# Dense products of a hybrid attention block: high and low parts in half precision with scaled weights, in place of a rounded 32-bit type

## The chip, the cores and the metric

The kernel runs on one core of a Trainium2 chip. The metric is the time of one execution on the device, in microseconds. Three runs of the kernel before took 1757.48, 1761.77 and 1765.3 us; the median, 1761.77, is the time before. A trace of one execution is read beside it.

A core has five engines that work at the same time, each through its own list of instructions in order: TensorE (matmul, PE in the profile, with its weight loads as PEld), VectorE (DVE), ScalarE (ACT), GpSimd (POOL) and SyncE (SP), which here issues the DMAs. They wait for each other through semaphores. SBUF holds the operands, and matmuls write to PSUM, which has eight banks of 512 columns in 32-bit.

## The reference

One layer of a block with two branches over 1024 tokens of width 1024, in 32-bit arithmetic. Cut to what matters here:

```
h = rms_norm(x, norm_mix)
u = h @ w_in                                  # 1024 x 5144 columns
q, kc, vc, ks, vs, kw, vw, gl, rw, merge = split(u)
o_nsa  = nsa(q, kc, vc, ks, vs, kw, vw, gl)   # attention: compressed, selected, window
o_rwkv = rwkv7(rw)                            # token shift, then a scan over the tokens
g = sigmoid(merge)
y = g[0] * (o_nsa @ proj_nsa) + g[1] * (o_rwkv @ proj_rwkv)
x = x + y @ w_out
n = rms_norm(x, norm_ffn)
a, b = split(causal_conv3(n @ ffn_up))        # 5632 columns, depthwise, three taps
x = x + (silu(a) * b) @ ffn_down              # 2816 rows
```

The dense products are `@ w_in`, the two projections, `@ w_out`, `@ ffn_up` and `@ ffn_down`.

## The kernel before, in words

**How a dense product is made.** Activations lie transposed, 128 channels on the partitions and 512 tokens (one half of the sequence) along the columns. Both operands of a product are split: `hi` is the value rounded to FR, a rounded 32-bit type that TensorE takes in a single pass, and `lo` is what is left over, again in FR. A product is then three passes, hi x hi, hi x lo and lo x hi, added up in one PSUM bank (`mm3`, line 263; `mm3s`, line 272, does two outputs at once). For 1024 input channels that is 3 x 8 = 24 matmuls of 128 x 128 weights by 512 columns per output group of 128 and half.

**Splitting.** ACT copies the 32-bit tile to `hi`; VectorE or POOL subtracts `hi` from the tile to make `lo`. `wload` (line 249) does this for weights: it loads a raw tile of 128 x 1024, ACT makes whi (line 256), and line 258 makes wlo, on VectorE, because the counter `wk` never leaves the range `WK = (0, 200)`. In the FFN, `wraw` (line 1561) loads a raw tile into one of four buffers in turn and `split8` (line 1567) and `cut` (line 1721) split it, mostly on POOL (lines 1572 and 1723).

**The stages, in order of time.**
- To about 60 us: x is loaded, normed (`normed`, line 238) and split into hhi and hlo for both halves; the first two column groups of w_in are loaded.
- To about 690 us: attention (`attention`, line 542). Keys are made and compressed (`kphase`), the values in natural order by `vnat` (line 497, matmuls at line 512 of 280 columns), then for every head the scores (lines 580, 641, 643), the exponentials (lines 650 and 651) and the product with the values (lines 655 to 660). The attention's own operands are half precision already. Between its steps the fillers are put: `zproj` and `mproj`, the other column groups of w_in (line 268), and `prelude`, which prepares the scan.
- To about 1000 us: the scan of the second branch, in eight units of 128 tokens (`front` and `back`), in 32-bit. Its steps wait for each other, and a list of dense work is put between them: the rest of `mproj`, `nproj` and `rproj` (the projections), `wout0` (w_out for the first half), `norm0`, and `ffn0` (the first FFN columns for the first half).
- To about 1215 us: the same for the second half, `gated` at line 1446, w_out at line 1473, and six FFN column pairs (i below NE = 6) with `mm3`.
- To about 1524 us: the other 16 column pairs. Here a 2 x 2 scheme with seven products instead of eight is used for the two halves and the two halves of the channels (`prod`, line 1633: twelve matmuls at line 1636 per product, 84 per pair). `prep_up` (line 1587) makes sums of raw weights on VectorE (lines 1592 to 1598) and splits them. Results are combined by VectorE (lines 1665 to 1682), convolved (`taps`, line 1500: an ACT eviction at line 1502, then VectorE at line 1505) and gated (`silu`, lines 1513 to 1515).
- To the end: the down projection, in five `plain` steps of two row groups (line 1746) and three `combined` steps of four (seven products again, line 1817). Each result is added from PSUM to a running sum by VectorE (`tick`, lines 1748 and 1826).

**What sets the order.** The program is written against a tile framework, which lays down the instructions of each engine in one list by simulated time and by priorities. `tc.cur_priority` gives the attention or the scan the first claim and the fillers the later ones; `tc.issue_after` forces single instructions behind others. `ps` (line 211) hands out PSUM banks by tag: P, M, A and B have two each. A tile with a tag and `bufs=n` waits for the last reader of the tile that had its place n tiles ago.

Of the kernel before, what the change touches and what calls it, by code (L numbers as in the profile page):

```python
# [54 lines left out]
NPOOL = ()  # L55
# [26 lines left out]
      "hlo_5", "hlo_6", "hlo_7")  # L82
CW = -0.5 * float(np.exp(-0.5))
# [83 lines left out]
def build(tc, D, dbg=None, upto=99):  # L167
# [7 lines left out]
    with ExitStack() as ctx:  # L175
# [14 lines left out]
        load(par, D["par"])  # L190

# [24 lines left out]
        def ktiles(p, name):  # L216
            return [p.tile([128, 512], FR, name=f"{name}_{k}", tag=f"{name}_{k}") for k in range(8)]
# [20 lines left out]
        def normed(h, xs, gname, rstd, hi, lo, tmp):  # L238
            for k in range(8):
# [3 lines left out]
                (G if k in NPOOL else V).tensor_sub(ks_(lo[h], k), hf, ks_(hi[h], k).bitcast(F32))  # L243
# [86 lines left out]
        V.tensor_scalar(pd[:, 26:30], par[:, o:o + 4], -0.5, 1.0, op0=ALU.mult, op1=ALU.add)  # L330
        ast = ExitStack()
# [74 lines left out]
        def kphase():  # L406
# [24 lines left out]
            for kv in range(2):  # L431
# [4 lines left out]
                def ev(h, pj):  # L436
                    for g in range(2):
                        for r in range(2):
                            dst = zp[g][64 * r:64 * r + 64, :, 1 + 32 * h:33 + 32 * h]
                            src = pj[64 * g:64 * g + 64].rearrange("p (n l r) -> p l n r", l=8, r=2)[:, :, :, r]  # L440
                            if r == g:
                                A.activation(dst, src, AF.Copy)
                            else:
                                V.tensor_copy(dst, src)
# [52 lines left out]
        def vnat():  # L497
# [3 lines left out]
            wnh = tmp.tile([128, 8, 280], FR, name="wnh", tag="wnh")  # L501
            wnl = tmp.tile([128, 8, 280], FR, name="wnl", tag="wnl")
            A.activation(wnh, wn, AF.Copy)
            G.tensor_sub(wnl, wn, wnh.bitcast(F32))
            for t in range(8):
# [8 lines left out]
                for j, vt in ((0, Vs), (1, Vw)):  # L514
                    src = pn[:, 128 * j:128 * j + 128].rearrange("p (g d) -> p g d", g=2)
                    A.activation(vt[:, t, :, 0:64], src, AF.Copy)
                    V.tensor_sub(vt[:, t, :, 65:129], src, vt[:, t, :, 0:64])
                A.activation(gat[:, t], pn[:, 256:280], AF.Exp, scale=-1.0)
# [167 lines left out]
        def zproj(gi):  # L686
            last = FP["f"].tile([128, 1], F32, name="zlast", bufs=2)

            def ev(h, pj):
                z = FP["f"].tile([128, 512], F32, name="zs", bufs=NZS)  # L690
                A.activation(z, pj, AF.Copy, scale=pd[:, gi:gi + 1])
                V.scalar_tensor_tensor(z[:, 1:512], pj[:, 0:511], P("mu", gi), z[:, 1:512],  # L692
# [3 lines left out]
                else:  # L696
                    V.scalar_tensor_tensor(z[:, 0:1], last, P("mu", gi), z[:, 0:1], op0=ALU.mult, op1=ALU.add)
# [20 lines left out]
        def reload(src):  # L718
            hi, lo = ktiles(FP["h"], "hhi"), ktiles(FP["h"], "hlo")
            for k in range(8):  # L720
# [3 lines left out]
                V.tensor_sub(lo[k], t, hi[k].bitcast(F32))  # L724
# [27 lines left out]
        def oprep():  # L752
            ob["hi"] = [FP["h"].tile([128, 512], FR, name=f"ohi{k}", tag=f"hhi_{k}") for k in range(4)]
            ob["lo"] = [FP["h"].tile([128, 512], FR, name=f"olo{k}", tag=f"hlo_{k}") for k in range(4)]
# [4 lines left out]
            for k in range(4):  # L759
# [3 lines left out]
                V.tensor_sub(ob["lo"][k], t, ob["hi"][k].bitcast(F32))  # L763
# [23 lines left out]
        def ysplit(m):  # L787
            def half(tag, name):
                p, n = (FP["f"], {"fu": 3}.get(tag, 1)) if tag in ("fu", "yx") else (FP["h"], 1)
                return p.tile([128, 512], FR, name=f"{name}{m}", tag=tag, bufs=n)  # L790
# [19 lines left out]
        def wout0(m):  # L810
# [5 lines left out]
            V.scalar_tensor_tensor(xr, pj, 0.5, xr, op0=ALU.mult, op1=ALU.add)  # L816
# [12 lines left out]
        def norm0():  # L829
# [10 lines left out]
            for n, k in enumerate(NK):  # L840
                hi[k], lo[k] = (FP["h"].tile([128, 512], FR, name=f"h2{c}0_{k}", tag=HT[2 * n + x]) for x, c in enumerate("hl"))
# [9 lines left out]
                los.append(V.tensor_sub(lo[k], t, hi[k].bitcast(F32)).ins)  # L851
# [576 lines left out]
        yhi = yp.tile([128, 8, 512], FR, name="yhi")  # L1428
# [504 lines left out]
```

## Time and profile before

| | |
|---|---|
| runs, us | 1757.48, 1761.77, 1765.3 (median 1761.77) |
| profiled execution | span 1754.8 us from the first to the last instruction; the page gives no further time of its own for it |
| instructions | 30772 |
| TensorE clock granted, mean | 0.996 |
| DMA | 224.65 MB, mean 128 GB/s |
| HBM | 153.86 MB read, 63.96 MB written |

How to read it. Times are microseconds unless marked ns. In a row of a group stand the line of the code, the engine, the operation, the tile written and the tiles read, the shapes, the count; then the busy time in all and the mean ns of one; then the idle time of the engine just before those instructions and what ended it. In the chain of waits, each row is a start, a length and a group that followed without a gap; the chain is followed back from the last instruction. In the table by stretches each row gives the busy time of each engine between two moments, with the number of instructions in brackets, then the granted clock, the share of the DMA engines and GB/s. Matmuls are pipelined and their ends are modelled: a matmul's own length is longer than the step from its start to the next start, so a pace is read from starts. The type FR is shown as f32 where a matmul reads it and as fp32r where an engine writes it; F16 is f16.

### The profile page before, as it was taken

The page shows a single profiled execution, that of the slowest core. Times are in us where ns is not written, and L with a number is a line of the kernel's source. Part 1 is how long each engine was busy: PE and PEld are TensorE (multiplying, and loading weights), DVE is VectorE, ACT ScalarE, POOL GpSimd, SP SyncE. Part 2 cuts the span into 40 slices and gives each one's busy share as a digit, 9 for nine tenths or more (in the row PEclk, how much of TensorE's full clock was granted, in tenths as well). Part 3 has the DMA queues.
Part 4 walks back from the last instruction along what each step waited for, and adds up shares of the span by engine and source line. Part 5 has one row for each costly group of instructions (what it writes and reads, how often), then busy time and mean ns, then how long its engine had stood idle before and what let it go on. Part 6 is the DMA issues. An engine that isn't in the chain of part 4 may idle for free.

```text
span 1754.8 us, 30772 instructions
## 1 busy us (share of the span) xinstructions
PE 1719.2 (98%) x11856; PEld 1344.9 (77%) x11856; DVE 1249.7 (71%) x2197; ACT 892.5 (51%) x1605; POOL 482.6 (28%) x349
## 2 busy tenths in 40 slices
PE   8999999999999999999999999999999999999998
PEld 5777667766777778887877878787888888888886
DVE  6445677778766648764547585499988888875798
ACT  6574675657557654446545563454344344534430
POOL 1101121120211220010003200113444444757857
PEclk9999999999999999999999999999999999999999
DMA  6242243331343455445445753443222222723402
GB/s 209 91 131 99 76 153 115 103 103 56 117 155 124 133 171 177 140 126 163 149 154 183 257 203 126 132 157 131 90 73 85 94 74 84 243 71 119 132 13 108
DMA packets 124690, 224.65 MB, mean 128 GB/s; under 512 B 16384, under 2 KB 45440, under 8 KB 124416
## 3 DMA queue, kind: packets, MB, share of 16 engines
q1 hardware_dynamic: 124544, 222.69, 39.1%
q8 instruction: 93, 1.52, 0.4%
q14 instruction: 53, 0.43, 0.1%
HBM read 153.86 MB, written 63.96 MB: 124 GB/s over the span
## 4 chain that ended last, share of the span: by engine, by line
PE 81%; DVE 9%; ACT 4%; DMA 4%; issue 2%; SPq 0%; DVEq 0%; ACTq 0%
PE psP L268 25%; PE psM L1636 7%; PE psA L1636 5%; PE psP L1636 5%; PE psA L268 4%; PE psB L268 2%; PE psP L288 2%; PE psM L268 2%; PE psA L641 2%; PE psM L1746 2%; PE psP L1746 2%; PE psA L1746 2%; PE psB L1746 2%; PE psA L643 2%; PE psM L580 1%
## 5 line engine op out<-in xcount | busy, mean ns | idle before, releaser
L268 PE MATMUL psP<-hhi,whi 128*128 128x512 f32 x560 | 227.7, 407 | 0.9 <-DVE zs L692 0.6
L268 PE MATMUL psP<-hlo,whi 128*128 128x512 f32 x560 | 225.4, 403 | 1.7 <-DVE hlo L243 1.7
L258 DVE TENSOR_TENSOR wlo<-wraw,whi 128x1024 fp32r<-128x1024 f32 (+1 forms) x98 | 113.7, 1161 | 73.1 <-ACT whi L256 39.6
L652 DVE TENSOR_TENSOR pl<-pf,ph 128x512 f16<-128x512 f32 (+3 forms) x208 | 118.7, 579 | 60.1 <-ACT pf L651 58.7
L268 PE MATMUL psP<-hhi,wlo 128*128 128x512 f32 x560 | 154.4, 404 | 0.0
L256 ACT ACTIVATE whi<-wraw 128x1024 fp32r<-128x1024 f32 (+1 forms) x98 | 93.0, 953 | 92.1 <-PE psP L268 43.3
L650 ACT ACTIVATE ph<-psA 128x512 f16<-128x512 f32 (+3 forms) x208 | 99.4, 478 | 73.1 <-PE psA L645 43.6
L268 PEld LDWEIGHTS psP<-hhi,whi 128*128 128x128 f32 x560 | 105.4, 188 | 25.1 <-DVE zs L692 1.4
L268 PEld LDWEIGHTS psP<-hlo,whi 128*128 128x128 f32 x560 | 105.5, 188 | 24.8 <-DVE hlo L243 2.7
L587 DVE TENSOR_REDUCE mp<-psM 128x1 f32<-128x512 f32 (+2 forms) x192 | 96.1, 516 | 33.2 <-PE psM L585 25.9
L268 PEld LDWEIGHTS psP<-hhi,wlo 128*128 128x128 f32 x560 | 102.4, 188 | 21.3 <-issue 0.5
L1572 POOL TENSOR_TENSOR wlo<-wraw,whi 128x1024 fp32r<-128x1024 f32 (+1 forms) x33 | 68.1, 2064 | 142.9 <-PE psA L268 46.3
L651 ACT ACTIVATE pf<-psA 128x512 f32<-128x512 f32 (+3 forms) x208 | 99.9, 480 | 0.0
L655 PEld LDWEIGHTS <-ph 128*128 128x128 f16 x592 | 55.8, 96 | 19.6 <-issue 9.3
L660 PEld LDWEIGHTS <-pl 128*128 128x128 f16 x592 | 54.9, 98 | 18.2 <-issue 6.2
L1372 POOL TENSOR_TENSOR b<-b,bonus 128x512 f32<-128x512 f32 x8 | 10.4, 1299 | 203.0 <-ACT b L1370 199.6
L1572 POOL TENSOR_TENSOR s34l<-s,s34h 128x1024 fp32r<-128x1024 f32 x16 | 38.6, 2413 | 93.4 <-ACT s34h L1571 89.9
L674 POOL TENSOR_TENSOR onat<-onat,ot 128x256 f32<-128x256 f32 x32 | 28.1, 885 | 122.6 <-DVE ot L673 85.8
L1515 DVE SCALAR_TENSOR_TENSOR th<-th,u 128x512 f32<-128x512 f32 x38 | 59.5, 1566 | 0.1
L658 PEld LDWEIGHTS <-ph 128*128 128x128 f16 x592 | 56.1, 97 | 2.4 <-issue 1.7
L1571 ACT ACTIVATE whi<-wraw 128x1024 fp32r<-128x1024 f32 (+1 forms) x38 | 33.5, 880 | 42.3 <-PE psP L1636 28.6
L1636 PE MATMUL psP<-h2h,whi 128*128 128x512 f32 x128 | 50.1, 391 | 1.2 <-ACT p L1662 1.2
(819 smaller groups left out, 5124.6 us busy)
## 6 DMA issues: line engine op xcount, KB each, us to landing
wraw<-f_up SPq DMA_DIRECT2D x56, 512.0 KB, 3.5
wraw<-w_t SPq DMA_DIRECT2D x46, 512.0 KB, 3.9
wraw<-f_dn SPq DMA_DIRECT2D x22, 512.0 KB, 4.0
th_d<-th SPq DMA_DIRECT2D x38, 256.0 KB, 2.2
sg_d<-zs SPq DMA_DIRECT2D x32, 256.0 KB, 2.3
wraw<-w_out SPq DMA_DIRECT2D x16, 512.0 KB, 3.4
z_d<-zs SPq DMA_DIRECT2D x28, 256.0 KB, 3.7
x<-xT SPq DMA_DIRECT2D x24, 256.0 KB, 5.9
```

The costliest lines, as they stand in the source:

```text
L256: A.activation(hi[:, :nk], raw, AF.Copy)
L258: (V if WK[0] <= wk[0] < WK[1] else G).tensor_sub(lo[:, :nk], raw, hi[:, :nk].bitcast(F32))
L268: lastm[0] = T.matmul(ps, a[:, k], ks_(b, k), start=(n == 0), stop=(n == 3 * nk - 1)).ins
L587: V.reduce_max(mp[:, x, br, t:t + 1], pm[:, 0:(b1 - b0) * 128], axis=AX.X)
L650: A.activation(ph[0:nkey, rg], pa[0:nkey, rg], AF.Exp, scale=0.125)
L651: A.activation(pf[0:nkey, rg], pa[0:nkey, rg], AF.Exp, scale=0.125)
L652: V.tensor_sub(pl[0:nkey, rg], pf[0:nkey, rg], ph[0:nkey, rg])
L658: T.matmul(pov[:, t, 0:64], ph[0:nkey, tk], vt[0:nkey, kb, g, 65:129], start=False, stop=False, skip_group_check=True)
L1515: V.scalar_tensor_tensor(th, th, 0.5, ub, op0=ALU.mult, op1=ALU.mult)
L1572: e.tensor_sub(lo[:, ks], raw[:, ks], hi[:, ks].bitcast(F32))
L1636: T.matmul(bank, w[wi][:, o_ + k], xs_[k][xi], start=start and n == 0, stop=n == 11, skip_group_check=True)
L1746: T.matmul(pj, x[:, m], y, start=(n == 0), stop=(n == 5))
```

## The change

The `hi` and `lo` tiles of all dense products become half precision (F16) in place of FR; the three passes stay. The weights are multiplied by `WS = 256` ahead of the split, and the products are multiplied by `WI = 1/256` where they leave PSUM or where the next parameter is applied. The small products of `loraproj` stay in FR, and the 32-bit products of the scan stay as they are.

The type itself, at every tile of this kind (here one of them):

```
-            return [p.tile([128, 512], FR, name=f"{name}_{k}", tag=f"{name}_{k}") for k in range(8)]
+            return [p.tile([128, 512], F16, name=f"{name}_{k}", tag=f"{name}_{k}") for k in range(8)]
...
-                (G if k in NPOOL else V).tensor_sub(ks_(lo[h], k), hf, ks_(hi[h], k).bitcast(F32))
+                (G if k in NPOOL else V).tensor_sub(ks_(lo[h], k), hf, ks_(hi[h], k))
```

Weights in `wload`, where the scale goes into the two instructions that are there:

```
-            hi = t_.tile([128, n, 128], FR, name="whi", bufs=2)
-            lo = t_.tile([128, n, 128], FR, name="wlo", bufs=2)
+            hi = t_.tile([128, n, 128], F16, name="whi", bufs=2)
+            lo = t_.tile([128, n, 128], F16, name="wlo", bufs=2)
             raw = t_.tile([128, n, 128], F32, name="wraw", bufs=2)[:, :nk]
             lastw[0] = load(raw, src).ins
-            A.activation(hi[:, :nk], raw, AF.Copy)
+            A.activation(hi[:, :nk], raw, AF.Copy, scale=WS)
             wk[0] += 1
-            (V if WK[0] <= wk[0] < WK[1] else G).tensor_sub(lo[:, :nk], raw, hi[:, :nk].bitcast(F32))
+            V.scalar_tensor_tensor(lo[:, :nk], raw, WS, hi[:, :nk], op0=ALU.mult, op1=ALU.subtract)
```

Weights in the FFN's `wraw` and in `vnat`, where the scale is an instruction of its own; the splits behind it lose only their bitcast:

```
             raw = (wp, fp)[rn_[0] // 2 % 2].tile([128, 8, 128], F32, name="wraw", bufs=2)
             lastw[0] = load(raw, src).ins
+            A.activation(raw, raw, AF.Copy, scale=WS)
             return raw
...
+            G.tensor_scalar(wn, wn, WS, 0.0, op0=ALU.mult, op1=ALU.add)
             A.activation(wnh, wn, AF.Copy)
-            G.tensor_sub(wnl, wn, wnh.bitcast(F32))
+            G.tensor_sub(wnl, wn, wnh)
```

The way back: parameters that follow a product are scaled once, and where there is no parameter the evacuating instruction gets the factor.

```
+        V.tensor_scalar(mus, par[:, o:o + 14], WI, None, op0=ALU.mult)
+        V.tensor_scalar(pd[:, 0:14], pd[:, 0:14], WI, None, op0=ALU.mult)
+        for q_ in ("gain", "conv"):
+            o, n_ = PAR[q_]
+            V.tensor_scalar(par[:, o:o + n_], par[:, o:o + n_], WI, None, op0=ALU.mult)
...
-            A.activation(sq[:, :n], px, AF.Square)
+            A.activation(sq[:, :n], px, AF.Square, scale=WI)
...
+            V.tensor_scalar(cw2[:, 0], cw2[:, 0], WS, None, op0=ALU.mult)
...
-                A.activation(sg, pj, AF.Copy)
+                A.activation(sg, pj, AF.Copy, scale=WI)
...
-            A.activation(hi, ob["y"][m], AF.Copy)
-            V.tensor_sub(lo, ob["y"][m], hi.bitcast(F32))
+            A.activation(hi, ob["y"][m], AF.Copy, scale=WI)
+            V.scalar_tensor_tensor(lo, ob["y"][m], WI, hi, op0=ALU.mult, op1=ALU.subtract)
...
-            V.scalar_tensor_tensor(xr, pj, 0.5, xr, op0=ALU.mult, op1=ALU.add)
+            V.scalar_tensor_tensor(xr, pj, 0.5 * WI, xr, op0=ALU.mult, op1=ALU.add)
...
-                    tick(V.tensor_add(acc[m, h], acc[m, h], pj))
+                    tick(V.scalar_tensor_tensor(acc[m, h], pj, WI, acc[m, h], op0=ALU.mult, op1=ALU.add))
```

More of the change, by code (lines that the diff above doesn't have):

```diff
@@ L82 @@
       "hlo_5", "hlo_6", "hlo_7")
+WS = 256.0
+WI = 1.0 / WS
 CW = -0.5 * float(np.exp(-0.5))
@@ L190, in build @@
         load(par, D["par"])
+        mus = cp.tile([128, PAR["mu"][1]], F32, name="mus")
         def P(name, j=0):
@@ L500, in vnat @@
             load(wn, D["w_n"])
-            wnh = tmp.tile([128, 8, 280], FR, name="wnh", tag="wnh")
-            wnl = tmp.tile([128, 8, 280], FR, name="wnl", tag="wnl")
+            wnh = tmp.tile([128, 8, 280], F16, name="wnh", tag="wnh")
+            wnl = tmp.tile([128, 8, 280], F16, name="wnl", tag="wnl")
+            G.tensor_scalar(wn, wn, WS, 0.0, op0=ALU.mult, op1=ALU.add)
             A.activation(wnh, wn, AF.Copy)
-            G.tensor_sub(wnl, wn, wnh.bitcast(F32))
+            G.tensor_sub(wnl, wn, wnh)
             for t in range(8):
@@ L515, in vnat @@
                     src = pn[:, 128 * j:128 * j + 128].rearrange("p (g d) -> p g d", g=2)
[L516 to L518 removed]
+                    A.activation(vt[:, t, :, 0:64], src, AF.Copy, scale=WI)
+                    V.scalar_tensor_tensor(vt[:, t, :, 65:129], src, WI, vt[:, t, :, 0:64], op0=ALU.mult,
+                                           op1=ALU.subtract)
+                A.activation(gat[:, t], pn[:, 256:280], AF.Exp, scale=-WI)
             V.tensor_scalar(gat, gat, 1.0, None, op0=ALU.add)
@@ L691, in ev @@
                 A.activation(z, pj, AF.Copy, scale=pd[:, gi:gi + 1])
-                V.scalar_tensor_tensor(z[:, 1:512], pj[:, 0:511], P("mu", gi), z[:, 1:512],
+                V.scalar_tensor_tensor(z[:, 1:512], pj[:, 0:511], mus[:, gi:gi + 1], z[:, 1:512],
                                        op0=ALU.mult, op1=ALU.add)
@@ L696, in ev @@
                 else:
-                    V.scalar_tensor_tensor(z[:, 0:1], last, P("mu", gi), z[:, 0:1], op0=ALU.mult, op1=ALU.add)
+                    V.scalar_tensor_tensor(z[:, 0:1], last, mus[:, gi:gi + 1], z[:, 0:1], op0=ALU.mult, op1=ALU.add)
                 nc.sync.dma_start(z_d[gi][:, H[h]], z)
@@ L752, in oprep @@
         def oprep():
-            ob["hi"] = [FP["h"].tile([128, 512], FR, name=f"ohi{k}", tag=f"hhi_{k}") for k in range(4)]
-            ob["lo"] = [FP["h"].tile([128, 512], FR, name=f"olo{k}", tag=f"hlo_{k}") for k in range(4)]
+            ob["hi"] = [FP["h"].tile([128, 512], F16, name=f"ohi{k}", tag=f"hhi_{k}") for k in range(4)]
+            ob["lo"] = [FP["h"].tile([128, 512], F16, name=f"olo{k}", tag=f"hlo_{k}") for k in range(4)]
             ob["y"] = [FP["h"].tile([128, 512], F32, name=f"y0_{m}", tag=f"{('hhi', 'hlo')[m // 4]}_{4 + m % 4}")
@@ L840, in norm0 @@
             for n, k in enumerate(NK):
-                hi[k], lo[k] = (FP["h"].tile([128, 512], FR, name=f"h2{c}0_{k}", tag=HT[2 * n + x]) for x, c in enumerate("hl"))
+                hi[k], lo[k] = (FP["h"].tile([128, 512], F16, name=f"h2{c}0_{k}", tag=HT[2 * n + x]) for x, c in enumerate("hl"))
                 if k > 3:
@@ L1451, in build @@
                 load(x2[m], D["xT"][m][:, H[1]])
-            A.activation(yhi[:, m], yt, AF.Copy)
-            V.tensor_sub(ylo[:, m], yt, yhi[:, m].bitcast(F32))
+            A.activation(yhi[:, m], yt, AF.Copy, scale=WI)
+            V.scalar_tensor_tensor(ylo[:, m], yt, WI, yhi[:, m], op0=ALU.mult, op1=ALU.subtract)
         ost.close()
@@ L1564, in wraw @@
             lastw[0] = load(raw, src).ins
+            A.activation(raw, raw, AF.Copy, scale=WS)
             return raw
@@ L1710, in pset @@
                 tags = ["T%d%s%d" % ((2, 1, 4)[p // 4], c, p % 4) for c in "hl"]
-                r.append([tf(t).tile([128, 512], FR, name="hh" + t[2], tag=t) for t in tags])
+                r.append([tf(t).tile([128, 512], F16, name="hh" + t[2], tag=t) for t in tags])
             return r
@@ L1717, in slot @@
             if n % 2 == 0:
-                return [wp.tile([128, 8, 128], FR, name=t, bufs=2) for t in ("whi", "wlo")]
-            return [fp.tile([128, 8, 128], FR, name=t) for t in (("s12h", "s12l"), ("s34h", "s34l"))[n // 2]]
+                return [wp.tile([128, 8, 128], F16, name=t, bufs=2) for t in ("whi", "wlo")]
+            return [fp.tile([128, 8, 128], F16, name=t) for t in (("s12h", "s12l"), ("s34h", "s34l"))[n // 2]]
         def cut(dst, src, e):
             A.activation(dst[0], src, AF.Copy)
-            e.tensor_sub(dst[1], src, dst[0].bitcast(F32))
+            e.tensor_sub(dst[1], src, dst[0])
         def plain(i0):
```

45 lines of the change are left out of this document (23 added, 22 removed).

## The prediction

> **What bounds the kernel now.** I read the page from the top: busy time by engine, the clock and the chain that ended last.
>
> ```profile
> PE 1719.2 (98%) x11856; PEld 1344.9 (77%) x11856; DVE 1249.7 (71%) x2197; ACT 892.5 (51%) x1605; POOL 482.6 (28%) x349
> PEclk9999999999999999999999999999999999999999
> PE 81%; DVE 9%; ACT 4%; DMA 4%; issue 2%; SPq 0%; DVEq 0%; ACTq 0%
> ```
>
> TensorE is busy 98% of the span, its clock is whole in every slice, and it makes 81% of the chain that ended last. An average can hide a stage with another limit, so next comes the table by stretches (columns: us, then busy time of PE, PEld, DVE, ACT, POOL with instruction counts, then clock, DMA share, GB/s).
>
> ```profile
> 60.00:690.00 630.00, 617.51 (x5037) 457.04 (x5036) 415.82 (x888) 382.44 (x804) 101.41 (x104) 1.00 0.38 120
> 690.00:1000.00 310.00, 304.29 (x3355) 246.81 (x3353) 184.12 (x375) 163.32 (x286) 42.34 (x30) 0.98 0.51 164
> 1000.00:1215.00 215.00, 211.77 (x915) 171.16 (x913) 160.25 (x227) 105.78 (x152) 27.50 (x13) 1.00 0.47 154
> 1215.00:1524.00 309.00, 307.30 (x1342) 251.60 (x1341) 269.32 (x406) 134.14 (x184) 146.53 (x68) 1.00 0.30 96
> 1524.00:1755.00 231.00, 225.51 (x977) 182.53 (x975) 183.95 (x242) 73.90 (x125) 155.84 (x104) 1.00 0.31 104
> ```
>
> TensorE leads everywhere. VectorE is second: 269.32 of 309 us (87%) where 16 of the FFN's column pairs are formed (1215 to 1524), 80% in the down projection. There the faster TensorE has the least room.
>
> A busy time is no pace, because matmuls overlap. The pace is in the chain's merged rows and in the starts of single matmuls.
>
> ```profile
> 1316.91 2.73 PE psP L1636 x12
> 640.22 17.14 PE psP L268 x74
> 130.63 3.14 PE psA L512 x24
> 561.63 0.20 PE L658 MATMUL psB<-Vw,ph 128*128 128x64 f16 x1
> 561.67 0.71 PE L268 MATMUL psP<-hhi,wlo 128*128 128x512 f32 x2
> 562.22 0.39 PE L268 MATMUL psP<-hhi,whi 128*128 128x512 f32 x1
> 564.25 0.38 PE L641 MATMUL psA<-qd,k1c 128*128 128x512 f16 x1
> 564.47 0.38 PE L643 MATMUL psA<-q,k2c 128*128 128x512 f16 x1
> 564.68 0.38 PE L645 MATMUL psA<-cb,identm 128*128 128x512 f16 x1
> ```
>
> The dense matmuls (shown as f32; their type is the rounded 32-bit one) follow each other every 2.73/12 = 227.5 ns in the FFN stage and every 17.14/74 = 231.6 ns among the fill of the attention. The attention's own half-precision matmuls of the same 128x512 shape, each with its own weights, start at 564.25, 564.47 and 564.68: 215 ns apart. That difference is the heart of the forecast: same array, same clock, same column count, 12.5 ns less.
>
> **The change part by part.** *Matmul pace.* The counts, by line, over the whole span:
>
> ```profile
> 0.00:1755.00 1755.00, 723.16 (x2904) 534.66 (x2904) 1.00 0.40 128
> 0.00:1755.00 1755.00, 68.81 (x264) 48.81 (x264) 1.00 0.40 128
> 0.00:1755.00 1755.00, 308.49 (x1344) 252.16 (x1344) 1.00 0.40 128
> 0.00:1755.00 1755.00, 111.99 (x480) 89.89 (x480) 1.00 0.40 128
> 0.00:1755.00 1755.00, 116.47 (x504) 94.33 (x504) 1.00 0.40 128
> ```
>
> They are lines 268, 288, 1636, 1746 and 1817: 5496 matmuls of 512 columns change type. The number of passes stays three. In the FFN lines the pace gain is 227.5 - 215 = 12.5 ns; 2328 x 12.5 = 29 us. For lines 268 and 288 the same floor gives 12.5 and the fill's pace gives 231.6 - 215 = 16.6; part of the latter is waiting that stays, so I take 14: 3168 x 14 = 44 us (bounds 40 and 53). The 192 matmuls of line 512 (280 columns) run every 3.14/24 = 131 ns. Scaling the half-precision pace by columns gives 215 x 280/512 = 118, so 192 x 13 = 2.5 us.
>
> *Weight loads.* Each matmul has one load:
>
> ```profile
> L268 PEld LDWEIGHTS psP<-hhi,whi 128*128 128x128 f32 x560 | 105.4, 188 | 25.1 <-DVE zs L692 1.4
> L655 PEld LDWEIGHTS <-ph 128*128 128x128 f16 x592 | 55.8, 96 | 19.6 <-issue 9.3
> ```
>
> 188 ns against 96. Behind a 512-column matmul a load of 188 ns is hidden already. Behind a short one it is not: the short matmul at 561.63 is followed by two dense ones, and the next dense one starts only at 562.22. Two at 227.5 ns after a 33 ns matmul would have ended at 562.12, so 0.1 us was exposed. Going through the matmuls in order I count 139 places where a dense one follows an attention matmul, with 0.06 to 0.1 us each: 8 to 14 us, and none of it goes if the load isn't the reason. I take 8.
>
> The Trainium skill speaks against all of this: the page "TensorE: Matmul & The Clock Gate", section "Weight-path perf modes — Fast Weight Load (FWL) and DoubleRow", says that the array handles one element per cell and cycle whatever the element's width, and that a load scales with columns and not with bytes. By that sentence the pace gain would be 0 and only the added work would be left. The trace differs: 227.5 against 215 ns, and 188 against 96; the measurement decides.
>
> TensorE's sum: 29 + 44 + 2.5 + 8 = 83 us.
>
> *Splitting weights.* In wload the scale rides on the ACT copy and the subtraction becomes one scalar_tensor_tensor. The choice of G was never taken (the count stays below 200), so the engine stays VectorE. Two-input VectorE instructions cost the same in both kinds and with a half-precision result:
>
> ```profile
> L816 DVE SCALAR_TENSOR_TENSOR xr<-psP,xr 128x512 f32<-128x512 f32 x8 | 5.5, 687 | 5.2 <-PE psP L268 5.0
> L537 DVE TENSOR_TENSOR ql<-qn,qh 128x512 f16<-128x512 f32 x6 | 4.1, 686 | 1.3 <-ACT qh L536 1.3
> L1748 DVE TENSOR_TENSOR acc<-acc,psM 128x512 f32<-128x512 f32 x20 | 13.6, 680 | 4.6 <-PE psM L1746 4.1 <-DMA th_d<-th 0.5
> ```
>
> 687, 686 and 680 ns. So the ticks, ysplit, zproj, taps and wload stay as they are: 7 ns on some 130 ticks is 1 us on an engine that isn't the bound. The scaled parameters are four short VectorE instructions (mus, pd, two of par) while the x tiles are being loaded, and one for cw2 long ahead of its matmul: nothing, and without cover under 0.7 us each.
>
> *The added pass.* wraw now scales the raw tile in place on ACT before anything else reads it.
>
> ```profile
> L1571 ACT ACTIVATE s12h<-s 128x1024 fp32r<-128x1024 f32 x16 | 17.0, 1062 | 17.8 <-PE psA L1636 14.1 <-PE psM L268 2.3 <-PE psM L1636 1.3
> wraw<-f_up SPq DMA_DIRECT2D x56, 512.0 KB, 3.5
> wraw<-f_dn SPq DMA_DIRECT2D x22, 512.0 KB, 4.0
> ```
>
> 56 + 22 loads, less 12 that go through wload, are 66 tiles at 1.06 us: 70 us more ACT from about 1090 us on. Between 1215 and 1524 ACT has 134 us in 309; 32 of the 66 tiles lie there, so 168 us, 58% of a shorter stretch. Its cover is the raw ring: four buffers, loaded about one column pair (19 us) ahead, landing in 3.5 us. What stands behind a scale in ACT's order is an eviction (lines 1502, 1662) at most 1.06 us later, and VectorE's taps wait for that. If the cover failed at each of the two tiles of a pair, VectorE would have 16.8 + 2.1 = 18.9 us per pair (269.32/16 = 16.8), above the new TensorE time of 84 x 0.215 = 18.1 and a little below the old 84 x 0.2275 = 19.1. So its price lies between 0 and 16 x 0.8 = 13 us; I take 3, since ACT idles nearly half the time there. The line 512 stage also gets one POOL pass over 2240 columns before wnh and wnl.
>
> ```profile
> L512 PEld LDWEIGHTS psA<-wnl,hhi x64: 187/188/331, 114.0 to 162.4; 128*128 128x128 f32 x64
> L504 POOL TENSOR_TENSOR wnl<-wn,wnh x1: 5169/5169/5169, 63.9 to 63.9; 128x2240 fp32r<-128x2240 f32 x1
> ```
>
> wnl is made from 63.9 to 69.1 us and first read at 114.0, so a pass like it (5 us) costs nothing; without that cover, 5 us.
>
> *POOL's subtractions.* They now read and write halves. No POOL row here does that with two inputs; the nearest are these.
>
> ```profile
> L1572 POOL TENSOR_TENSOR s12l<-s,s12h 128x1024 fp32r<-128x1024 f32 x16 | 40.7, 2546 | 5.1 <-ACT s12h L1571 4.1 <-PE psM L268 1.1
> L413 POOL TENSOR_SCALAR cb<-cl 128x512 f16<-128x512 f32 x4 | 3.8, 960 | 18.2 <-DMA cl<-cst 18.0
> L1032 POOL TENSOR_SCALAR zs<-zs 128x512 f32<-128x512 f32 x16 | 10.5, 656 | 102.6 <-ACT zs L1025 101.4 <-ACT gat L518 0.5
> L912 POOL TENSOR_SCALAR kk<-zk,par 128x512 f32<-128x512 f32 x8 | 9.8, 1219 | 7.0 <-DMA zk<-z_d 6.3
> L1515 DVE SCALAR_TENSOR_TENSOR th<-th,u 128x512 f32<-128x512 f32 x38 | 59.5, 1566 | 0.1
> 1319.96 2.41 POOL L1572 TENSOR_TENSOR wlo<-wraw,whi 128x1024 fp32r<-128x1024 f32 x1 [3.87 <-ACT whi L1571]
> 1321.16 1.77 DVE L1515 SCALAR_TENSOR_TENSOR th<-th,u 128x512 f32<-128x512 f32 x1
> 1331.34 0.70 DVE L1678 TENSOR_TENSOR psA<-psA,u 128x512 f32<-128x512 f32 x1 [1.44 <-PE psA L1636]
> ```
>
> A half-precision result (960) lies between 656 and 1219 for full ones, so the factor is 0.8 to 1.5, and I take 1.0. It matters beyond POOL, since line 1515, two SBUF inputs on VectorE, takes 1566 ns where the like VectorE rows take 687. In the order of time POOL's wlo ends at 1322.37, and the VectorE instruction that began at 1321.16 ends 0.56 us after that, at 1322.93: it stood while POOL ran. So a slower POOL lengthens VectorE too. Below 1 would give VectorE room, worth at most what TensorE doesn't yet collect.
>
> *What isn't collected.* Per column pair VectorE's 16.8 us must fit into 18.1, so I leave 0.3 us per pair, 5 us. In the scan stage (690 to 1000) half the matmuls are the dense fill that covers the scan's own waits; with about 500 of them (by my count to 950 us) shorter by 14 ns, I leave half, 4 us. Start, the down projection's end and ACT's pass: 4 us. Together 13.
>
> **Sum.** 83 - 13 = 70 us. The profiled span is 1754.8 us; the page gives no time beside it, and the median of the runs, 1761.77, is 7 us above it. So the span goes to about 1685 and the time to 1762 - 70 = 1692 us.
>
> **The rivals.** *VectorE, with ACT and POOL, takes over after 1000 us.* For it: 87% busy, the blocked line 1515, the new ACT pass. Against: TensorE is still 7% longer per pair (18.1 to 16.8), and VectorE's longest wait in the pair after 1319 us, the 1.44 us ahead of line 1678 above, is for TensorE. All gain there (915 + 1342 + 977 = 3234 matmuls x 12.5 = 40 us) would go: 83 - 40 - 8 = 35 us, about 1727.
>
> *Halves are slow on POOL, and the kernel gets slower.* Place: lines 1572 and 1723. Price at a factor of 2: the down projection's 155.84 us become 312 against 231, so +81; between 1215 and 1524 two waits of VectorE per pair grow by 2.5 us each, 269 + 80 = 349 against 309, so +40; the gain ahead of 1000 us (about 44) stays: +77, about 1839. Solving both stretches for a net of zero, it decides from a factor of about 1.7. Against it: the 960 ns row.
>
> *The type doesn't set the pace.* If the 12.5 ns came from where the operands lie and not from their width, only ACT's pass (0 to 13 us) is left: 1762 to 1775. Against: the three rows at 564 us have the same weights and columns as the dense ones. This is what the Trainium skill's sentence above would make of it.
>
> *The planner orders the instructions anew.* It places them by simulated time, and the types change that. The place is the scan stage, with some 60 steps (eight units of about eight). A filler put behind a step and not ahead of it leaves TensorE waiting, as in the 0.3 to 0.7 us that single VectorE and ACT rows take; 0.3 to 0.6 at each step is 20 to 40 us: 1712 to 1732, with the pace gain still in it.
>
> **How the numbers follow.** Forecast 0.72, VectorE taking over 0.10, new order 0.08, POOL 0.06, type without effect 0.04. For the forecast itself: TensorE's terms lie between 69 + 0 = 69 and 29 + 53 + 2.5 + 14 = 98; what isn't collected lies between 0 and 30 (13 for ACT's cover, 16 x 0.6 for VectorE, 7 for the scan). That is 1664 to 1723. To hold 8 in 10 the range takes in VectorE's takeover and the new order: 1664 to 1736. Above it lie POOL and the type without effect (0.10), below it some 0.04. A measurement of this kernel can tell about 0.5%, 9 us, from no change. Faster by more: 0.90 (the first three). Within: 0.03 (most of the type without effect). Slower: 0.07 (POOL and a remainder).
>
> **What would show it.** Right: chain rows of twelve L1636 matmuls at about 2.58 us in place of 2.73; the loads of line 268 near 96 ns; the stretch of one column pair near 18.2 us in place of 19.2; POOL's lines 1572 and 1723 unchanged in length; ACT longer by about 70 us. The collected part is wrong where the chain after 1215 us turns from PE to DVE; the POOL term is wrong if s12l takes over 3.5 us; the whole is wrong if the dense pace stays at 227 ns.

## The result, and the profile after

The changed kernel takes 1734.97 us (median of four runs, 1732.74 to 1737.26) against 1760.99 us for the kernel before in the same session: a ratio of 0.9852 with a 95% interval of 0.983 to 0.9875. It is faster by 26 us. The forecast was 1692 us, so a gain of 70: the time lies at the upper end of the range of 1664 to 1736, and little more than a third of the gain came. The profiled execution has a span of 1731.9 us, 22.9 less than before.

The page of the changed kernel, top lines: busy time by engine, the clock, the chain that ended last, and the loads of line 271 (268 before) and the new pass.

```profile
PE 1646.6 (95%) x11856; PEld 862.9 (50%) x11856; DVE 1247.6 (72%) x2202; ACT 941.2 (54%) x1669; POOL 453.0 (26%) x350
PEclk9999999999999999999999999999999999999999
PE 37%; DVE 19%; DMA 6%; ACT 5%; issue 3%; SPq 0%; POOL 0%; DVEq 0%; ACTq 0%
L271 PEld LDWEIGHTS <-whi 128*128 128x128 f16 x1840 | 176.9, 98 | 209.7 <-issue 12.1
L1577 ACT ACTIVATE wraw<-wraw 128x1024 f32<-128x1024 f32 x66 | 69.7, 1056 | 141.5 <-DMA wraw<-f_up 96.3
```

TensorE was 81% of the chain and is 37%; VectorE, DMAs and ACT have come into it. The row of nines does not say that the clock was whole, since a nine stands for 90% or more; the mean over the run is 0.986, against 0.996 before. The weight loads are down from 188 to 98 ns. The last line is the one to stop at: the 66 passes cost 69.7 us as forecast, but ACT stood idle for 141.5 us just ahead of them, 96.3 of it until a load of an up weight landed.

The table by stretches of the changed kernel (columns as in the prediction):

```profile
690.00:1000.00 310.00, 291.02 (x3245) 182.57 (x3246) 185.16 (x377) 158.55 (x279) 42.21 (x30) 0.98 0.52 173
1000.00:1215.00 215.00, 208.76 (x950) 93.82 (x949) 166.72 (x248) 119.63 (x171) 29.57 (x14) 0.98 0.41 138
1215.00:1524.00 309.00, 287.88 (x1293) 127.93 (x1291) 266.78 (x382) 152.49 (x210) 132.49 (x70) 0.98 0.30 103
```

From 1215 to 1524 us TensorE does fewer matmuls than before (1293 against 1342), though each is faster: busy 287.88 where it was 307.30. No other engine is full there; VectorE is even less busy than before. That fits a loop of waits, not of an engine that has become the bound.

The length of the pair stage stands in the starts of one tile, first the kernel before, then the changed one:

```profile
L1636 PE MATMUL psP<-h2h,whi x128: 389/391/496, 1212.5 to 1509.9; 128*128 128x512 f32 x128
```

```profile
L1649 PE MATMUL psP<-h2h,whi x128: 379/379/631, 1180.4 to 1500.5; 128*128 128x512 f16 x128
```

297.4 us have become 320.1. The stage was reached 32.1 us earlier; all but a third of that is lost in it. Counted from every 84th matmul, a pair took 19.17 us before (the first 22.07). Now the first takes 27.13, the next four 18.13 each, which is 84 x 0.216, and then they go up: 19.73, 21.12, 22.70, 19.60, 22.54 and so on, 20.30 in the mean of pairs 2 to 15, against 19.18 before.

The chain of waits of the changed kernel in one of the long pairs (start, length, what):

```profile
1379.97 0.33 SPq L1528
...
1396.48 2.30 DVE th L1527
...
1398.95 2.38 DVE th L1527
1401.34 0.33 SPq L1528
...
1401.76 3.56 DMA wraw<-f_up
1405.41 1.06 ACT wraw L1577
1406.46 0.58 ACT u L1514
1407.07 0.76 DVE u L1517
```

No TensorE is in it. VectorE's last gate product of a pair releases its store, which SyncE has to issue; the next instruction in SyncE's list is the load of a raw tile; ACT waits for that load with its pass; behind the pass stands the eviction `u<-psB`; and for that eviction VectorE's taps wait, at whose end the next gate product stands. One turn, from store to store (1379.97 to 1401.34), is 21.4 us. In ACT's list the place of the pass changes in the course of the stage (timeline of ACT, changed kernel; the bracket is the idle time and what ended it):

```profile
1242.35 0.69 ACT L1514 ACTIVATE u<-psB,par 128x512 f32<-128x512 f32 x1 [5.35 <-DVE psB L1686]
1242.93 1.05 ACT L1584 ACTIVATE s34h<-s 128x1024 f16<-128x1024 f32 x1
1243.88 1.04 ACT L1577 ACTIVATE wraw<-wraw 128x1024 f32<-128x1024 f32 x1
...
1260.15 1.06 ACT L1577 ACTIVATE wraw<-wraw 128x1024 f32<-128x1024 f32 x1 [5.34 <-DMA wraw<-f_up]
1261.12 0.67 ACT L1514 ACTIVATE u<-psB,par 128x512 f32<-128x512 f32 x1
```

At 1243.88 the pass stands behind the eviction and waits for nothing. From 1260.15 on it stands ahead of it and ACT waits 5.34 us for the load (7.92 us at 1405.41). For the rest of the stage, over ten pairs in a row, ACT's list has the pass ahead of `u<-psB`. The first two of these passes (1260.15 and 1278.80, a wait of 5.34 us each) still lie in pairs of 18.13 us; from the third on the wait is 7.7 to 8.1 us and the pairs are long. The framework laid the list so; that its simulated times put the pass there is inferred, not shown.

### The profile page after: what moved, and what is told of

Its sections match the earlier page's. It is cut to its first block, busy times and chain, and to the rows that moved or that the text cites. A ratio compares the mean times of both kernels' runs of the same rounds, so it can differ in the third digit from the quotient of the medians.

```text
span 1731.9 us, 30712 instructions
## 1 busy us (share of the span) xinstructions
PE 1646.6 (95%) x11856; PEld 862.9 (50%) x11856; DVE 1247.6 (72%) x2202; ACT 941.2 (54%) x1669; POOL 453.0 (26%) x350
## 4 chain that ended last, share of the span: by engine, by line
PE 37%; DVE 19%; DMA 6%; ACT 5%; issue 3%; SPq 0%; POOL 0%; DVEq 0%; ACTq 0%
PE psP L271 10%; DVE u L1517 4%; DVE th L1527 3%; DMA wraw<-f_up 3%; PE psA L271 2%; PE psP L291 2%; PE psM L1759 1%; PE psP L1759 1%; PE psB L1759 1%; PE psM L1649 1%; PE psA L1759 1%; PE psM L271 1%; PE psP L1830 1%; DMA zs<-sg_d 1%; PE psA L1649 1%
## 5 line engine op out<-in xcount | busy, mean ns | idle before, releaser
L271 PEld LDWEIGHTS <-whi 128*128 128x128 f16 x1840 | 176.9, 98 | 209.7 <-issue 12.1
L271 PE MATMUL psP<-hlo,whi 128*128 128x512 f16 x560 | 212.2, 379 | 2.1 <-DVE hlo L246 2.1
L271 PE MATMUL psP<-hhi,whi 128*128 128x512 f16 x560 | 212.3, 379 | 2.0 <-ACT ad L973 1.5
L261 DVE SCALAR_TENSOR_TENSOR wlo<-wraw,whi 128x1024 f16<-128x1024 f32 (+1 forms) x98 | 112.0, 1143 | 62.5 <-ACT whi L259 38.2
L1577 ACT ACTIVATE wraw<-wraw 128x1024 f32<-128x1024 f32 x66 | 69.7, 1056 | 141.5 <-DMA wraw<-f_up 96.3
L271 PE MATMUL psP<-hhi,wlo 128*128 128x512 f16 x560 | 142.3, 381 | 0.0
L259 ACT ACTIVATE whi<-wraw 128x1024 f16<-128x1024 f32 (+1 forms) x98 | 92.8, 949 | 90.5 <-PE psP L271 46.5
L271 PEld LDWEIGHTS <-wlo 128*128 128x128 f16 x920 | 88.0, 98 | 100.0 <-issue 4.3
L1585 POOL TENSOR_TENSOR wlo<-wraw,whi 128x1024 f16<-128x1024 f32 (+1 forms) x33 | 58.2, 1765 | 162.1 <-ACT whi L1584 146.8
L1527 DVE SCALAR_TENSOR_TENSOR th<-th,u 128x512 f32<-128x512 f32 x38 | 69.1, 1818 | 0.5
L1649 PEld LDWEIGHTS <-whi 128*128 128x128 f16 x384 | 38.0, 99 | 49.2 <-issue 5.4
L1585 POOL TENSOR_TENSOR s34l<-s,s34h 128x1024 f16<-128x1024 f32 x16 | 34.6, 2164 | 101.1 <-ACT s34h L1584 101.1
```

The lines of the kernel that those rows point to most:

```text
L259: A.activation(hi[:, :nk], raw, AF.Copy, scale=WS)
L261: V.scalar_tensor_tensor(lo[:, :nk], raw, WS, hi[:, :nk], op0=ALU.mult, op1=ALU.subtract)
L271: lastm[0] = T.matmul(ps, a[:, k], ks_(b, k), start=(n == 0), stop=(n == 3 * nk - 1)).ins
L1527: V.scalar_tensor_tensor(th, th, 0.5, ub, op0=ALU.mult, op1=ALU.mult)
L1577: A.activation(raw, raw, AF.Copy, scale=WS)
L1585: e.tensor_sub(lo[:, ks], raw[:, ks], hi[:, ks])
```

## The experiments

Three theories stood against each other. **A**: the pass of ACT waits for a load at a bad place in ACT's list, and so closes the loop shown above. **B**: VectorE and POOL are what limits the pairs, since they hold each other up. **C**: the pass costs by its amount, 70 us of ACT. In all ratios the kernel before, run on the same chip in the same session, is 1.

**No pass at all.** The factor of 256 is left out (scale 1), so the weights are split as they are; the other instructions stay.

```
-WS = 256.0
+WS = 1.0
...
-            A.activation(raw, raw, AF.Copy, scale=WS)
```

> The scale is 1 instead of 256 and the in-place ACT pass over the FFN's raw weight tiles is gone; all else is as changed. Theory A (the pass waits for its load in ACT's order, and the evictions behind it wait with it): the 16 column pairs of the FFN go back to TensorE's pace, 18.1 to 18.4 us each instead of 20 to 22.7, the 1344 matmuls from 331 to about 300 us, and the kernel to about 1700 us. Theory B (VectorE is the limit there, held up by POOL at the shared SBUF access, and the pass is innocent): pairs stay at 19.5 us or more and the kernel above 1725.

Measured: 1706.8 us, ratio 0.9706 (0.9679 to 0.9734). After a first pair of 27.16 us all pairs take 18.13 (one 18.40). The chain of waits of this kernel in the same stretch has nothing but TensorE:

```profile
1386.77 2.59 PE psP L1648 x12
...
1392.81 4.32 PE psM L1648 x20
1397.13 2.59 PE psP L1648 x12
```

Twelve in 2.59 us, the forecast 2.58. So the pass costs the changed kernel some 26 us by the two ratios (0.9852 less 0.9706) and 29 us of the pair stage (330.9 against 301.5 us from the first to the last start), and halves can be had without it. A and C agree with this, B does not in its plain form.

**One pass of a pair moved.** All work as in the change, but one pass of each pair is ordered behind the eviction `u<-psB`.

```
+            if len(uev) > 1:
+                with tc.issue_after(uev[-2]):
+                    A.activation(raw, raw, AF.Copy, scale=WS)
...
-            taps(u[1][1], 1, i, 1, pd_, lambda d: pb[:, 512 - d:512])
+            uev.append(taps(u[1][1], 1, i, 1, pd_, lambda d: pb[:, 512 - d:512]))
```

> All passes stay, but of each pair one of the two is ordered behind an eviction of PSUM (u11) that it stood ahead of: one swap in ACT's order per pair and nothing else. Theory A: pairs fall to 18.1 to 18.8 us, the kernel to 1702 to 1712. Theory B, and theory C (the 70 us of extra ACT work cost by their amount, wherever they stand): pairs stay near 21 us, the kernel within 6 us of 1735.

Measured: 1714.27 us, 0.9745 (0.9712 to 0.9777). The first six pairs are as in the kernel without a pass, the later ones 18.1 to 20.4 us. One swap in ACT's list, with the same work, gives back some 19 us by the ratios. C falls with this. A had pairs of 18.1 to 18.8 us and 1702 to 1712, and the later pairs miss that, the time by 2 us. In the chain of these pairs the pass, though behind `u<-psB`, still stands ahead of `s34h` (the hi part of a weight sum), and POOL's `s34l` waits for that: one turn, from pass to pass (1395.11 to 1415.18), is 20.07 us.

**The pass on POOL.**

```
-            A.activation(raw, raw, AF.Copy, scale=WS)
+            G.tensor_scalar(raw, raw, WS, 0.0, op0=ALU.mult, op1=ALU.add)
```

> The pass moves from ACT to POOL (66 of about 1.0 us, from the 2.06 us that POOL took over 2240 columns). Theory A: evictions wait for no load any more, but POOL's subtractions do; pairs at 18.1 to 19, the kernel at 1700 to 1715. Theory B: VectorE is held up by 2 us more per pair, pairs at 21 us or more, the kernel at 1735 or above.

Measured: 1712.41 us, 0.9747 (0.9711 to 0.9783). The first pair takes 32.99 us, all others 18.13 but one of 18.99. The timeline of POOL in this kernel:

```profile
1385.72 1.04 POOL L1577 TENSOR_SCALAR wraw<-wraw 128x1024 f32<-128x1024 f32 x1 [3.68 <-DMA wraw<-f_up]
...
1392.83 1.23 POOL L1577 TENSOR_SCALAR wraw<-wraw 128x1024 f32<-128x1024 f32 x1 [1.43 <-DMA wraw<-f_up]
```

The pass waits for the loads here too, and it costs nothing in these pairs; on POOL no eviction stands behind it. From 1215 to 1480 us POOL is busy for 150.80 us and VectorE for 243.87, against 105.11 and 231.53 in the changed kernel, and the pairs are short: that the two are full is not what made the pairs of the changed kernel long, and B falls in that form. What it costs is 6 us more in the first pair.

**The same pass in the kernel before.** `A.activation(raw, raw, AF.Copy)` in place on the raw tiles, with the old type.

> The kernel before, with the rounded 32-bit type, and only an in-place ACT copy (no factor) of the FFN's raw weight tiles added. Theory A: the price depends on where the planner puts the copies: if ahead of the evictions, pairs go from 19.2 to about 21 us or more and the kernel to 1780 to 1800; if behind, within 5 us of 1761. Theory B: within 5 us of 1761. Theory C: 1761 plus a few us, with pairs evenly longer.

Measured: 1762.38 us, 1.0021 (1.0003 to 1.0039); pairs 19.30 us in the mean, 19.18 before, and the first 25.92 against 22.07. All three theories allowed this time, so the run does not part them. Here the framework put the pass directly ahead of `u<-psB` in three single pairs (1280.83, 1338.24 and 1453.21 us), where ACT waited 7.25, 4.44 and 6.11 us for the load; these pairs and the next ones took 19.18 to 20.04 us. So a single pass at a bad place was absorbed; what costs is one in pair after pair. The 66 passes of 1.06 us cost 0.5 to 7 us by the interval (1760 x 0.0003 and x 0.0039), which holds the 3 us of the prediction, as long as they do not stand badly in pair after pair.

**A third raw buffer in each pool.** If the cover is too short because a buffer comes free late, more buffers should help.

```
-            raw = t_.tile([128, n, 128], F32, name="wraw", bufs=2)[:, :nk]
+            raw = t_.tile([128, n, 128], F32, name="wraw", bufs=3)[:, :nk]
...
-            raw = (wp, fp)[rn_[0] // 2 % 2].tile([128, 8, 128], F32, name="wraw", bufs=2)
+            raw = (wp, fp)[rn_[0] // 2 % 2].tile([128, 8, 128], F32, name="wraw", bufs=3)
```

> The changed kernel with three raw buffers in each of the two pools in place of two; the pass of ACT stays, in the same number and size. Theory A (the pass waits for a load that is issued too late, behind the two stores of th on SyncE, since its buffer comes free late; the pass holds the eviction behind it in ACT's order, and so closes a loop through VectorE and SyncE): the loads go out about half a period earlier, most pairs come back to 18.1 us, the stretch from 1215 to 1524 us is near 302 to 308, and the time is 1705 to 1715. Theory B (VectorE and POOL, held on the same port, are full in these pairs, whatever the loads do): pairs stay at 19.4 to 21 us, 1725 to 1737.

Measured: 1736.2 us, 0.987 (0.9846 to 0.9894): no change. That is theory B's number, but the timeline shows another reason. SyncE in this kernel, then ACT:

```profile
1380.79 2.86 SPq L1528 DMA_DIRECT2D th_d<-th  x2
1383.74 0.38 SPq L175 DMA_DIRECT2D wraw<-f_up  x1
```

```profile
1387.33 1.06 ACT L1577 ACTIVATE wraw<-wraw 128x1024 f32<-128x1024 f32 x1 [7.86 <-DMA wraw<-f_up]
1388.29 0.67 ACT L1514 ACTIVATE u<-psB,par 128x512 f32<-128x512 f32 x1
```

The load is still the next instruction behind the two stores, and the pass is still ahead of the eviction. The order of ACT's and SyncE's lists in these pairs is the same as with two buffers. Theory A had a wrong half: not the buffers set the moment of the load and the pass, but the places that they have in two lists.

**The low parts of the up weights all on POOL, without the pass.** This is for the first pair, 27.16 us long without any pass; VectorE is busy without a break ahead of it.

```
-WV = (3, 99, 1)
+WV = (99, 99, 1)
```

> The kernel with a scale of 1 and no pass on raw tiles (the first experiment), and besides all low parts of the up weights made on POOL, none on VectorE. VectorE was busy without a break from about 1115 to 1195 us and the first column pair took 27.2 us, against 22.1 in the kernel before. If the subtractions on VectorE are what makes the first pair long: it comes to 20 to 23 us, and the time to 1699 to 1704. If it is the T splits and their releases, or POOL's own lateness: first pair 26 us or more, 1705 to 1709.

Measured: 1712.7 us, 0.9732 (0.971 to 0.9753). The first pair becomes longer, 31.0 us, and it begins 8 us later; the time lies above both ranges. Relieving VectorE was the wrong idea.

**Third buffer and all low parts on POOL, with the pass.** The two edits above together, on the changed kernel.

> The changed kernel with the scale of 256 and its pass, three raw buffers in each pool, and the low parts of the up weights all on POOL. If both causes are independent: the gain of the third buffer plus some 4 to 7 us of the first pair, about 1700 to 1709. If POOL, with more work, becomes the one that closes the loop: no better than the third buffer alone.

Measured: 1749.94 us, 0.9945 (0.9929 to 0.996), the worst of all with the new type: a first pair of 38.68 us, and the long pairs as in the change. That is 14 us above the third buffer alone.

**Third buffer without the pass.** The control for the two above.

> The kernel with a scale of 1 and no pass, with three raw buffers. This is the control for the third buffer: its pairs are at 18.1 us already, which is the pace of 84 matmuls at 215 ns, so theory A expects no change from the first experiment beyond 3 us (1704 to 1709). If a third buffer helps by something else than the pass's cover (the split's own wait for the load, say), it shows here as more than 5 us.

Measured: 1704.13 us, 0.9689 (0.9671 to 0.9707). The pairs stay at 18.13; the first one is 24.83 instead of 27.16 us. Nothing but the first pair gains, and the time is at the lower end of what was expected.

**Third buffer and both passes moved** behind `u<-psB` of the pair before the last one, which a third buffer allows.

> The changed kernel with three raw buffers per pool, as in the run before with a third buffer, and both passes of a pair ordered behind the eviction u<-psB of the pair before the last one. In ACT's order the stretch 'pass, whi, u<-psP, s12h, pass, u<-psB' of the changed kernel becomes 'whi, u<-psP, s12h, u<-psB, pass, pass'; count, size and engine of the passes stay. Theory A, narrowed (what costs is that ACT, which works in order, stands at a pass whose load has not landed, ahead of an eviction that VectorE waits for; the number of buffers alone does not move that place, so the third buffer alone did nothing): pairs at 18.1 us, th's last product (L1527) near 1.2 to 1.4 us in the mean, 1705 to 1712 us. Theory B (VectorE and POOL are full on their port with any pass): pairs at 19.4 us or more, above 1722 us.

Measured: 1714.07 us, 0.9743 (0.9728 to 0.9758). ACT does not wait for a load any more:

```profile
1394.72 0.69 ACT L1514 ACTIVATE u<-psB,par 128x512 f32<-128x512 f32 x1 [6.61 <-DVE psB L1692]
1395.31 1.99 ACT L1581 ACTIVATE wraw<-wraw 128x1024 f32<-128x1024 f32 x2
1397.20 0.59 ACT L1681 ACTIVATE p<-psP 128x512 f32<-128x512 f32 x1
```

Against the run with the third buffer alone, only this order differs, and 22 us come back. Pairs are between 18.13 and 19.28, and the time is 2 us above what A gave. The last gate product takes 1.39 us in the mean, as A had it. In the long pairs TensorE waits for VectorE's sum `q` (4.5 us in eight places); what makes that late wasn't settled.

**Two buffers, both passes moved** behind the latest `u<-psB` (`uev[-1]` in the edit above, for both).

> The changed kernel with its two raw buffers per pool, and both passes of a pair ordered behind the last eviction u<-psB that stands ahead of them in the program: ACT's order becomes 'whi, u<-psP, s12h, u<-psB, pass, pass, s34h'. Theory A, narrowed: the eviction is free of the load, but s34h and with it POOL's s34l now stand behind two loads that are issued behind the stores of th. Between the run that moved one pass (pairs of 18.1 to 20.4 us, 1714 us) and the third buffer with moved passes: 1708 to 1720 us. Theory B: 1725 us or more.

Measured: 1721.21 us, 0.9769 (0.9721 to 0.9818), just above the range that A gave, but the four runs lie between 1711.54 and 1728.98, so that is not clear; in the profiled one (1725.65) most pairs take 19.40 us. Now `s34h` stands behind the passes, and the chain of this kernel shows the loop that is left:

```profile
1402.08 1.99 ACT wraw L1581 x2
1404.07 0.95 ACT s34h L1590
...
1405.15 2.53 POOL s34l L1591
```

It is a loop again, though ACT waits for no load: the passes now delay `s34h`, that delays POOL's `s34l`, and VectorE's next sum waits for it.

**Two buffers, both passes behind `p1`**, ACT's first copy of a pair.

```
+            if uev:
+                with tc.issue_after(uev[-1]):
+                    A.activation(raw, raw, AF.Copy, scale=WS)
...
-            A.activation(p1, pa, AF.Copy)
+            uev.append(A.activation(p1, pa, AF.Copy).ins)
```

> The changed kernel with its two raw buffers, and both passes of a pair ordered behind the copy p1, which is the first ACT work of a pair: ACT's order becomes 'p1, pass, pass, u<-psM, s12h, whi, ...'. The same work at another place. Theory A, narrowed: if the loads have landed by then, the wait goes and pairs come to 18.1 us (1706 to 1712 us); if they have not, u<-psM, the eviction on which the two products th and their stores hang, stands behind them, and the loop is closed as before or worse, 20 us a pair or more (1730 us or more). Which one it is shows in ACT's idle time ahead of the pass. Theory B expects no dependence on the place: 1730 to 1737 us.

Measured: 1703.14 us, 0.9684 (0.9663 to 0.9706), 3 us below the range that A gave. All pairs but two take 18.13 us (the first 24.92, one 19.42). The starts of the tile from above, and ACT in this kernel:

```profile
L1655 PE MATMUL psP<-h2h,whi x128: 379/379/634, 1180.8 to 1469.9; 128*128 128x512 f16 x128
```

```profile
1391.85 0.58 ACT L1681 ACTIVATE p<-psP 128x512 f32<-128x512 f32 x1
1392.33 1.99 ACT L1581 ACTIVATE wraw<-wraw 128x1024 f32<-128x1024 f32 x2
1394.22 0.67 ACT L1514 ACTIVATE u<-psM,par 128x512 f32<-128x512 f32 x1
...
1404.18 0.69 ACT L1514 ACTIVATE u<-psB,par 128x512 f32<-128x512 f32 x1 [4.50 <-DVE psB L1692]
```

The row of the two passes has no bracket: their loads have landed. They too stand ahead of an eviction, `u<-psM`, but ACT waits for no load there. 289.1 us from first to last start, where the change has 320.1, with the same 66 passes on the same engine, the same buffers and the same scale. This version beats both kernels with the scale kept, 56 us below the kernel before (1759.23 in its session), and its ratio is that of the kernel without a pass and with three buffers (0.9689).

## Why the prediction was right or wrong

**Matmul pace: right.** Twelve dense matmuls now take 2.59 to 2.60 us, so 216 ns against the forecast 215; the 280-column ones start 119 ns apart (forecast 118). The Trainium skill's sentence in "TensorE: Matmul & The Clock Gate", section "Weight-path perf modes — Fast Weight Load (FWL) and DoubleRow", by which the width of an element does not matter, is not borne out by 227.5 against 216 ns. The table of the same section says that weights other than 32-bit ones can be loaded 32 bits at a time, measured there at about twice the rate; the trace agrees with that, 188 against 98 ns.

**Weight loads: right.** In the attention's fill the second dense matmul behind a short one is no longer late (timeline of TensorE, first the kernel before, then the changed one):

```profile
574.89 0.20 PE L658 MATMUL psB<-Vs,ph 128*128 128x64 f16 x1
574.92 0.47 PE L268 MATMUL psP<-hhi,whi 128*128 128x512 f32 x1
575.24 0.39 PE L268 MATMUL psP<-hlo,whi 128*128 128x512 f32 x1
```

```profile
518.64 0.19 PE L670 MATMUL psB<-Vw,ph 128*128 128x64 f16 x1
518.67 0.38 PE L271 MATMUL psP<-hhi,whi 128*128 128x512 f16 x1
518.88 0.38 PE L271 MATMUL psP<-hlo,whi 128*128 128x512 f16 x1
```

The step from the first dense one to the second is 0.32 us before and 0.21 after. Taken over all dense matmuls that follow an attention one and are followed by a dense one (113 before, 107 after), it went from 334 to 218 ns in the mean. Less the gain in pace, some 0.1 us at each, that makes about 11 us (an estimate), where the prediction took 8 of 8 to 14.

**POOL: right.** `s12l` takes 2499 ns (2546 before), `s34l` 2164 (2413): a factor of 0.90 to 0.98. The slow-POOL rival is out.

**The added pass: this is the step that failed.** The prediction gave it 3 us within 0 to 13, with "Its cover is the raw ring: four buffers, loaded about one column pair (19 us) ahead, landing in 3.5 us". At the place that it got, it costs 31 us: 330.9 us for the pair stage in the change (first to last start of line 1649) against 299.7 with the passes behind `p1`. The amount was right (69.7 us, forecast 70), and the amount alone costs little (0.2% in the old kernel). The cover was not there: the load goes out behind the two stores, and the pass stands where its load has not landed, ahead of an eviction. The bound failed with it. It added the 1.06 us of a pass to VectorE's busy time (16.8 + 2.1) and did not ask what ACT would wait for at that place. The wait was 5 to 8 us, and the sum of a loop's lengths, not an engine's busy time, sets the pair. The kernel before had both hints: raw loads and stores of `th` go through one list, SyncE's, and the pass goes into a list with evictions in it.

In that loop the lengthened gate product counts as well (VectorE, then POOL, changed kernel):

```profile
1271.65 0.68 DVE L1527 SCALAR_TENSOR_TENSOR th<-th,u 128x512 f32<-128x512 f32 x1
...
1272.50 2.37 DVE L1527 SCALAR_TENSOR_TENSOR th<-th,u 128x512 f32<-128x512 f32 x1
```

```profile
1272.07 2.25 POOL L1585 TENSOR_TENSOR wlo<-wraw,whi 128x1024 f16<-128x1024 f32 x1 [5.58 <-ACT whi L1584]
```

The first product starts ahead of POOL's instruction and takes 0.68 us. The second starts inside it and ends 0.55 us after POOL's end, so about as long as it takes alone. The Trainium skill, "SBUF — State Buffer", section "SBUF: two separate sides", says that VectorE with two SBUF inputs and GpSimd exclude each other for a whole instruction; these rows agree. This pair still takes 18.13 us; in the long ones both products are held (2.30 and 2.38 us in the chain above). The hold alone does not make a pair long: with the passes behind `p1` one product of most pairs is held for 2.37 us and the pairs take 18.13 us (1258 ns in the mean of all, 1818 in the change, 1566 before). But the two holds make 3.3 us of the turn of 21.4, and without them it would be about 18.1 us (an estimate from these rows), which is TensorE's pace. No run has the pass at its bad place and no hold, so whether the place would have cost as much without the hold is not shown. That the pass costs nothing at another place is shown.

**What isn't collected: too small ahead of 1000 us.** By the forecast the pair stage should have begun 50 us earlier (44 + 2.5 + 8, less 4 for the scan), and it began 32 us earlier, in the change and in the best version alike. What TensorE waited for from 690 to 1000 us, before and after:

```profile
PE psC L1143 <- DVE yc L1364: 1.9, 2, 1.0
PE psB L1334 <- DVE QE L1311: 1.6, 1, 1.6
```

```profile
PE psC L1155 <- DVE yc L1376: 4.1, 3, 2.5
PE psC L1357 <- DVE Send L1337: 3.8, 1, 3.8
PE psP L845 <- POOL sq L838: 2.0, 1, 2.0
```

All rows of this view add up to 5.6 us before and 18.5 after; from 0 to 660 us they are 18.4 and 30.1. That is 24.6 us of new waits, where the forecast had 4. The granted clock adds to it: up to the pair stage the traces have it at 0.50 for 13.7 us before and for 23.9 us after, up to 5 us of TensorE's time (an estimate, half of the difference). The prediction had read the clock as whole. The fill also moved: 723 dense matmuls lie between the first and the last step of the scan, 663 before. That is the rival of a new order in part, at the place that it named. Whether the order itself or the scan's own steps, which did not become faster, make these waits was not tried.

**The first pair.** It went from 22.07 to 27.13 us, which the prediction did not have. TensorE waits 4.3 us there for the split T1h (the hi part of a sum of activations) and 1.9 for p1, and the granted clock falls (the first pair by stretches, kernel before, then changed):

```profile
1212.49:1234.56 22.07, 20.37 (x86) 15.61 (x84) 20.42 (x32) 7.11 (x11) 9.91 (x3) 1.00 0.38 133
```

```profile
1180.41:1207.54 27.13, 20.89 (x86) 8.66 (x85) 21.86 (x37) 12.67 (x18) 8.96 (x4) 0.87 0.42 152
```

The clock is 0.50 from 1190.2 to 1197.0 us, just behind the first of the waits, and dense matmuls start every 0.43 us there in place of 0.216, which loses about 2.5 us. With the 6.2 us of waits and 18.13 us for the matmuls, that makes 26.9 of the 27.13 (an estimate from these rows). The third buffer without a pass or the passes behind `p1` bring it to 24.8 and 24.9, with the clock at 0.50 for 3.4 us; more work on POOL brings it to 31 and 38.7. Why T1h comes late was not settled, nor whether the wait is what lowers the clock.

**The sum.** 70, less 18 ahead of the pairs, 28 for the pass (31 against 3) and some 4 for the first pair (24.9 with the passes behind `p1`, where about 21 was due), is 20; the span fell by 22.9. The down projection gave 9.7 us of its 12 (230.3 to 220.6 us). The chain after 1215 us turned from PE to DVE, which the prediction had named as the sign that its collected part is wrong. The rival of VectorE taking over had that sign and the wrong mechanism: VectorE is busy for 266.78 us of 309, less than before. That its 1727 us lies nearer to the measured time than the forecast is luck. So is it that the time lies inside the range: the forecast's own terms ended at 1723, and the rest up to 1736 was put there for two rivals.

## What to carry to other kernels

An instruction added to an engine that is half idle is not free by that: look at what it will wait for and at what stands behind it in the same list, above all an eviction or a split that another engine waits for. Check the cover of a load at its issue, by the instruction ahead of it on the issuing queue, and not by the number of buffers. Where busy times of all engines fall and the stage gets longer, look in the chain for a loop through two queues; moving one instruction in one list can be worth more than the engine time of all of them (here 31 us for an order; 70 us of work cost at most 7 us in the old kernel).

## What was not expected of the hardware

- A dense matmul of 512 columns with its own weights starts every 227.5 ns in the rounded 32-bit type and every 216 ns in half precision (pair stage, granted clock 1.00 from 1215 to 1524 us in the kernel before and in the one without a pass); 280 columns go from 131 to 119 ns. So the difference is about 12 ns at both sizes.
- POOL's one-input pass over 128 x 1024 took 1.04 us (in the run with the pass on POOL) and its two-input subtraction of the same size 2.13, about twice as long.
